# Delta rule with a convolution as side work: whose queue stores and loads, and how many steps lie between

## The chip, the cores and the metric

The kernel runs on one core of one Trainium2 chip. The metric is device time of one launch in microseconds; the times of the kernel before are the median of three runs. A trace comes from one further execution, taken with the hardware profiler. PE is TensorE, DVE VectorE, ACT ScalarE, POOL GpSimd, and SP SyncE, which here only issues transfers.

## What is computed

A trunk of two layers over 512 latent tokens (x) and 256 context tokens (ctx), 1024 wide, in float32: each layer is half a SwiGLU block, a mixer, and half a SwiGLU block. The first layer's mixer holds what the change touches: a convolution module beside a gated delta rule in both directions.

```
h    = a * sigmoid(g)                             # 512 channels
h    = depthwise_conv(h, conv_w)                  # 31 taps; latents in rows of 64 tokens
conv = silu(layer_norm(h + conv_b, ln_g, ln_b))

# delta rule, 4 heads of 128, chunks of 64 tokens, forward and backward
a_mat = where(strict, einsum(k * beta, k) * decay, 0)
t_mat = triangular_solve(a_mat + eye, eye)        # the inverse of a unit triangular matrix
v_new = u - w @ S ;  S = S * exp(g_last) + k_tail^T @ v_new ;  o = qd @ S + qk @ v_new
```

## The kernel before

One program is written out by hand. Each engine takes its instructions in the order in which the Python code emits them, and waits by semaphores for what an instruction reads. Weights come from memory through SP's queue into three raw buffers; most matrix products are split into a high and a low part and run as three matmuls.

The convolution works on four blocks (m = 0 to 3) of 128 channels. A block is a row of 918 elements: eight rows of 64 latent tokens with 15 zeros between them, then the 256 context tokens. `conv31` makes 31 taps: the first are accumulated by DVE in `ca` (L854, L857), the others are scaled by ACT (L860, L866) and added by POOL in `cp` (L845, L861, L867); at the end DVE adds both (L871) and `ca`, 888 wide with its padding, goes to the DRAM buffer `cD` (L872). It is a generator: each `yield` ends one step.

Blocks 0 and 1 run beside the projections (`conv_taps` takes some steps at the end of each projection). Blocks 2 and 3 are parked in `hD` and run as side work of the delta rule, in `side_work`: load the block (L1459, L1465), two steps, the steps of `conv31`. Then three passes over the four blocks follow (`each`): sums for the mean, centring with squares, and scaling with silu. The first two load from `cD` and pick the tokens out of the padding, in two transfers (L1446 with runs of 64 elements, L1447).

The delta rule (`gdn_ticks`) works on six chunk pairs t, two directions d and two head pairs hp. For each there are three generators:

- `prep(t, d, hp)`: the decay matrix (L1217, an exponential L1219), key and query products (L1222), the matrix N (L1227, L1230), its diagonal blocks (L1233), the first step of the inverse as a mask product and a subtraction from the identity (L1236, L1237, on DVE or POOL, with L1238 on POOL), and the transpose of that on PE (L1243), copied by ACT (L1244).
- `levels(t, d, hp)`: five doublings of the inverse: matmul, copy by ACT (L1255, L1256), a mask product by POOL (L1258), matmul, subtraction by DVE (L1266, L1269); then the last one (L1273 to L1282).
- `scan(t, d)`: the state S and the output `o_acc` of one chunk pair.

`run` advances them: in one tick every generator makes one step, in order, then the side work makes one. A first run prepares t = 0 alone. The phase t = -1 has levels(0) and prep(1); the phases t = 0 to 3 have scan(t), levels(t + 1) and prep(t + 2); the last has scan(4) and levels(5). A phase has 13 ticks. In the phases with a scan the first two preparations join at tick AFT, the other two at the tick after. Between the ticks stand matrix products of the adaptive modulation (L434, L496), whose weights SP loads (L445, L490).

Of the kernel before, what the change touches and what calls it, by code (L numbers as in the profile page):

```python
# [9 lines left out]
F32 = mybir.dt.float32  # L10
# [6 lines left out]
P = 128  # L17
# [4 lines left out]
NT = NX + NCTX  # L22
# [13 lines left out]
TAPU = 8  # L36
NLAST = 6
STG = 2
AFT = 5
NG = 3  # L40
NBG = 4
S5RD = 3
# [17 lines left out]
def trunk_kernel(  # L60
# [26 lines left out]
    def PS(name):  # L87
        return psum.tile([P, 512], F32, tag="ps", name=name)
# [708 lines left out]
    CW = 888  # L797
    NPOOL, NPOOL2 = TAPS[:2]
    hD = dram.tile([2, P, HW], F32, name="hD")
    cD = dram.tile([4, P, CW], F32, name="cD")  # L800
    sgD = dram.tile([4, P, NT], F32, name="sgD")
    kD = dram.tile([6, P, 512], F32, name="kD")
    vD = dram.tile([6, P, 512], F32, name="vD")
# [34 lines left out]
    def conv31(m, hb, ca, cp, ct):  # L838

        w = lambda j: cwT[:, j * 4 + m:j * 4 + m + 1]  # L840
        n = NPOOL if ct is not None else NPOOL2
        pj = list(range(31 - n, 31))
        cps = cp if isinstance(cp, list) else [(cp, 0, CW)]
        for c_, a, b in cps:
            GP.tensor_scalar(c_, hb[:, pj[0] + a:pj[0] + b], w(pj[0]), par[:, CONVB_O + m:CONVB_O + m + 1], ALU.mult, ALU.add)  # L845
        k = 1
        while ct is not None and k < n:
            for c_, a, b in cps:
                GP.tensor_scalar(ct[:, a:b], hb[:, pj[k] + a:pj[k] + b], w(pj[k]), None, ALU.mult)
                GP.tensor_tensor(c_, c_, ct[:, a:b], ALU.add)  # L850
            k += 1
        if ct is not None:
            yield
        V.tensor_scalar(ca, hb[:, 0:CW], w(0), None, ALU.mult)  # L854
        yield
        for j in range(1, 31 - n):
            V.scalar_tensor_tensor(ca, hb[:, j:j + CW], w(j), ca, ALU.mult, ALU.add)  # L857
            while k < n and k * (31 - n) < j * n:
                t = tmp.tile([P, SAW], F32, tag="sa", name="ctt")
                SC.activation(t, hb[:, pj[k]:pj[k] + CW], AF.Copy, scale=w(pj[k]))  # L860
                GP.tensor_tensor(cp, cp, t, ALU.add)  # L861
                k += 1
            yield
        while k < n:
            t = tmp.tile([P, SAW], F32, tag="sa", name="ctt")
            SC.activation(t, hb[:, pj[k]:pj[k] + CW], AF.Copy, scale=w(pj[k]))  # L866
            GP.tensor_tensor(cp, cp, t, ALU.add)  # L867
            k += 1
            yield
        for c_, a, b in cps:  # L870
            V.tensor_tensor(ca[:, a:b], ca[:, a:b], c_, ALU.add)  # L871
        nc.sync.dma_start(cD[m], ca)  # L872
        yield

    def conv_taps(n, tick=lambda: None):
# [267 lines left out]
    def gdn_ticks():  # L1143
# [60 lines left out]
        def prep(t, d, hp):  # L1204
            cp = ORDER[d][t]
            cols = slice(cp * P, (cp + 1) * P)
            col = lambda a, h: a[:, cp * 8 + d * 4 + 2 * hp + h:cp * 8 + d * 4 + 2 * hp + h + 1]
            DT, N, VV, Vc, bl = wk(t, d, hp)
            Ns, Nc, Vv, Vt = DT[:, :128], DT[:, 128:], Vc[:, :128], Vc[:, 128:]
            Pt = Ps[d][t % 2][:, hp * 256:hp * 256 + 256]  # L1210
            bg = DT
            if t == 0:
                bg = PS("growbc")
                for h in range(2):
                    mm(bg[:, hs(h)], col(cst[:, G], h).to_broadcast([P, P]), ident, start=True, stop=True)
            for h in range(2):
                V.scalar_tensor_tensor(DT[:, hs(h)], bg[:, hs(h)], col(cst[:, G], h), neg[:, d], ALU.subtract, ALU.min)  # L1217
            yield
            SC.activation(DT, DT, AF.Exp)  # L1219
            b0 = PS("gq")  # L1220
            for h in range(2):
                mm(b0[:, h * 256:h * 256 + 256].rearrange("p (a f) -> p a f", a=2),  # L1222
                   qk[:, 4 + 2 * hp + h, cols], qk[:, 2 * hp + h:2 * hp + h + 5:4, cols], start=True, stop=True)
            yield
            for h in range(2):
                o = h * 256
                V.scalar_tensor_tensor(N[:, hs(h)], b0[:, o + P:o + 2 * P], col(sc[:, BRK2], h), DT[:, hs(h)], ALU.mult, ALU.mult)  # L1227
            for h in range(2):
                o = h * 256
                V.scalar_tensor_tensor(Pt[:, hs(h)], b0[:, o:o + P], col(cst[:, RK], h), DT[:, hs(h)], ALU.mult, ALU.mult)  # L1230
            yield
            for q in quad:
                SC.copy(H2(Nc)[q], H2(N)[q, :, q])  # L1233
            yield
            E = V if t == 0 or hp == 0 else GP
            E.tensor_tensor(H2(Vv), H2(Nc), bl(0), ALU.mult)  # L1236
            E.tensor_tensor(H2(Vv), eye.unsqueeze(1).to_broadcast([P, 2, 64]), H2(Vv), ALU.subtract)  # L1237
            GP.tensor_tensor(H2(Ns), H2(Nc), bl(1), ALU.mult)  # L1238
            yield
            bt = PS("vt")  # L1240
            for h in range(2):
                for q in quad:
                    mm(ch(bt, h)[q], ch(Vv, h)[q], ident[q, q], start=True, stop=True)  # L1243
            SC.copy(Vt, bt[:, :128])  # L1244
            yield
# [191 lines left out]

    def side_work(cvs, cp):

        def load(m, src=None):  # L1440
            t = tmp.tile([P, SAW], F32, tag="sa", name="lnc")
            if src is not None:
                SC.dma_start(t[:, :NT], src[m])
                return t
            b = bass.AP(tensor=cD.tensor, offset=cD[m].offset, ap=[[CW, P], [79, 8], [1, 64]])
            SC.dma_start(t[:, XS].rearrange("p (r w) -> p r w", w=64), b)  # L1446
            SC.dma_start(t[:, CS], cD[m, :, 632:888])  # L1447
            return t

        def each(fn, src=None):  # L1450

            nxt = load(0, src)
            yield
            yield
            for m in range(4):
                t, nxt = nxt, load(m + 1, src) if m < 3 else None
                yield from fn(m, t)
        hb, ca = cvs
        nc.sync.dma_start(hb, hD[0])  # L1459
        yield  # L1460
        yield
        for m in (2, 3):
            yield from conv31(m, hb, ca, cp, None)
            if m == 2:
                nc.sync.dma_start(hb, hD[1])  # L1465
                yield
                yield

        def add(m, t):
            if m == 0:  # L1470
                GP.tensor_copy(acc[:, :NT], t[:, :NT])
            else:
                V.tensor_tensor(acc[:, :NT], acc[:, :NT], t[:, :NT], ALU.add)
            yield
            yield
        yield from each(add)
        for z in ("x", "c"):
            s, _ = STR[z]
            ps = PS("lnm")[:, :s.stop - s.start]
            mm(ps, ones, acc[:, s], start=True, stop=True)  # L1480
            yield
            SC.activation(rst[:, s], ps, AF.Copy, scale=1.0 / 512)

        def centre(m, t):
            V.tensor_tensor(t[:, :NT], t[:, :NT], rst[:, :NT], ALU.subtract)
            yield
            SC.dma_start(nD[m], t[:, :NT])
            q = cvs[m % 2]
            SC.activation(acc[:, :NT] if m == 0 else q[:, :NT], t[:, :NT], AF.Square)
            yield  # L1490
            if m:
                V.tensor_tensor(acc[:, :NT], acc[:, :NT], q[:, :NT], ALU.add)
        yield from each(centre)
        for z in ("x", "c"):
            s, _ = STR[z]
            n = s.stop - s.start
            ps = PS("lnv")
            mm(ps[:, :n], ones, acc[:, s], start=True, stop=True)
            yield
            rsqrt_newton(rst[:, s], ps[:, :n], 1.0 / 512, n, cvs)  # L1500

        def scaled(m, t):
            V.tensor_tensor(t[:, :NT], t[:, :NT], rst[:, :NT], ALU.mult)
            yield
            SC.activation(t[:, :NT], t[:, :NT], AF.Silu, bias=par[:, CLNB_O + m:CLNB_O + m + 1], scale=par[:, CLNG_O + m:CLNG_O + m + 1])
            SC.dma_start(nD[m, :, XS], t[:, XS])
            yield
            hi, lo = T["xnc"]
            split(hi[:, m], lo[:, m], t[:, CS])
        yield from each(scaled, nD)  # L1510
        def gates(h):
            sg = tmp.tile([P, SAW], F32, tag="sa", name="hsg")[:, :NCTX]
            SC.dma_start(sg, sgD[h, :, CS])
            return sg
        sgs = [gates(0), gates(1)]
        yield
        yield
        for h in range(4):
            sg = sgs[h]
            head_out("c", h, (4, 5), sg)  # L1520
            if h < 2:
                sgs.append(gates(h + 2))
            yield
            yield
# [762 lines left out]
```

## Time and profile before

| | |
|---|---|
| median of three runs | 2989.99 us (2988.91 to 2992.88) |
| profiled execution | 2993.55 us |
| its span, first to last instruction | 2991.8 us |
| busy: PE, DVE, ACT, POOL | 2832.5, 2005.1, 1112.4, 1087.0 us |
| PE's mean granted clock | 0.963 of full speed |
| the delta rule's stage | about 893 to 1192 us of the span |

Busy times are those of the instructions of an engine; DMA-issuing instructions and waits are not among them. A row of the timeline gives start, length, engine, line, operation, what it writes and reads, how many it merges, and in brackets the idle time of the engine ahead of it with what ended it. ACTq and SPq are the queues on which ACT and SP issue transfers. A granted clock of 1.00 is 2.4 GHz, one of 0.50 is 1.2 GHz.

### The profile page before, as it was taken

Reading aid. Unit: us, or ns where it says so; the run is one execution under the profiler, and the core shown is the slowest. Engines: PE = TensorE matmul, PEld = TensorE weight load, DVE = VectorE, ACT = ScalarE, POOL = GpSimd, SP = SyncE. Lnnn points to the kernel's source line nnn. Section 1 sums busy time; section 2 is a strip of 40 time slices with the busy share of each in tenths; the row PEclk is TensorE's granted clock in tenths of the full one; section 3 lists DMA queues with packets and bytes.
Section 4 is the critical chain, followed back from the end, with each engine's and each line's share of the span. In section 5 each row is a group of like instructions: output and inputs, shape, how many; then the busy total and the mean of one; then the engine's idle time right before and its main releaser. Section 6 shows DMA issues by size and latency. Waiting matters only on the chain.

```text
span 2991.8 us, 53430 instructions
## 1 busy us (share of the span) xinstructions
PE 2832.5 (95%) x21247; PEld 2520.0 (84%) x21247; DVE 2005.1 (67%) x3817; ACT 1112.4 (37%) x2311; POOL 1087.0 (36%) x1232
## 2 busy tenths in 40 slices
PE   7899999998997899999999999999999989899998
PEld 5799999977885677888888889799999977678997
DVE  4665666667857667658666576766666656588887
ACT  4233333343444435432222233433333332344444
POOL 0242333339307833002655232443333300046653
PEclk9899999998897898999999999999999989899999
DMA  6323341221234584332333211122221226433331
GB/s 228 104 73 127 99 127 57 65 72 43 75 106 158 200 261 150 128 83 76 105 101 103 99 54 54 50 71 62 67 76 60 71 66 211 162 105 100 113 99 64
DMA packets 306104, 308.34 MB, mean 103 GB/s; under 512 B 35053, under 2 KB 261513, under 8 KB 299200
## 3 DMA queue, kind: packets, MB, share of 16 engines
q1 hardware_dynamic: 284592, 274.89, 28.8%
q10 hardware_dynamic: 20256, 25.76, 2.6%
q8 instruction: 167, 2.74, 0.4%
q0 software_dynamic: 1008, 4.29, 0.4%
q14 instruction: 81, 0.66, 0.1%
HBM read 279.34 MB, written 25.56 MB: 102 GB/s over the span
## 4 chain that ended last, share of the span: by engine, by line
PE 73%; DVE 13%; ACT 4%; DMA 2%; POOL 2%; issue 2%; SPq 0%; ACTq 0%; POOLq 0%; DVEq 0%
PE s L369 7%; PE s L373 7%; PE s L371 7%; PE sc L371 3%; PE sc L369 3%; PE sc L373 3%; DVE wlo L163 2%; PE b L1266 1%; DVE nt L321 1%; DVE hT L688 1%; PE uac L373 1%; PE uac L371 1%; PE uac L369 1%; PE uax L369 1%; PE uax L371 1%
## 5 line engine op out<-in xcount | busy, mean ns | idle before, releaser
L163 DVE TENSOR_TENSOR wlo<-raw,whi 128x512 fp32r<-128x512 f32 (+1 forms) x793 | 596.1, 787 | 300.3 <-ACT whi L162 287.5
L162 ACT ACTIVATE whi<-raw 128x512 fp32r<-128x512 f32 (+1 forms) x813 | 476.0, 617 | 687.7 <-PE sc L371 122.4
L369 PE MATMUL s<-xnhx,whi 128*128 128x256 f32 x976 | 277.0, 284 | 0.0
L371 PE MATMUL s<-xnlx,whi 128*128 128x256 f32 x976 | 276.3, 283 | 0.4 <-DVE xnlx L364 0.4
L373 PE MATMUL s<-xnhx,wlo 128*128 128x256 f32 x976 | 276.2, 283 | 0.0
L659 POOL TENSOR_TENSOR gl<-sa,gh 128x256 fp32r<-128x256 f32 x122 | 95.8, 805 | 331.0 <-ACT gh L658 331.0
L373 PE MATMUL s<-xt,wlo 128*128 128x256 f32 x732 | 207.4, 283 | 1.8 <-POOL wlo L163 1.8
L369 PE MATMUL s<-xt,whi 128*128 128x256 f32 x732 | 207.1, 283 | 0.0
L371 PE MATMUL s<-xt,whi 128*128 128x256 f32 x732 | 207.1, 283 | 0.0
L578 POOL TENSOR_TENSOR raw<-raw 128x512 f32<-128x512 f32 x61 | 82.1, 1346 | 311.8 <-issue 286.5
L369 PEld LDWEIGHTS s<-xnhx,whi 128*128 128x128 f32 x976 | 187.2, 192 | 7.6 <-DVE hT L688 3.4
L369 PE MATMUL sc<-xnhc,whi 128*128 128x256 f32 x672 | 190.2, 283 | 0.0
L371 PE MATMUL sc<-xnlc,whi 128*128 128x256 f32 x672 | 190.2, 283 | 0.0
L373 PE MATMUL sc<-xnhc,wlo 128*128 128x256 f32 x672 | 190.1, 283 | 0.0
L371 PEld LDWEIGHTS s<-xnlx,whi 128*128 128x128 f32 x976 | 187.2, 192 | 1.5 <-DVE xnlx L364 0.6
L373 PEld LDWEIGHTS s<-xnhx,wlo 128*128 128x128 f32 x976 | 187.2, 192 | 0.0
L373 PEld LDWEIGHTS s<-xt,wlo 128*128 128x128 f32 x732 | 140.5, 192 | 2.0 <-POOL wlo L163 2.0
L369 PEld LDWEIGHTS s<-xt,whi 128*128 128x128 f32 x732 | 140.5, 192 | 0.0
L371 PEld LDWEIGHTS s<-xt,whi 128*128 128x128 f32 x732 | 140.5, 192 | 0.0
L369 PEld LDWEIGHTS sc<-xnhc,whi 128*128 128x128 f32 x672 | 129.0, 192 | 0.0
L371 PEld LDWEIGHTS sc<-xnlc,whi 128*128 128x128 f32 x672 | 129.0, 192 | 0.0
L373 PEld LDWEIGHTS sc<-xnhc,wlo 128*128 128x128 f32 x672 | 129.0, 192 | 0.0
(760 smaller groups left out, 8403.1 us busy)
## 6 DMA issues: line engine op xcount, KB each, us to landing
raw<-in_ffn_w_dram SPq DMA_DIRECT2D x176, 512.0 KB
raw<-in_w_mod_dram SPq DMA_DIRECT2D x64, 1024.0 KB
raw<-in_ffn_w_dram SPq DMA_DIRECT2D x32, 1024.0 KB
raw<-in_ffn_w_dram SPq DMA_DIRECT2D x16, 768.0 KB
raw<-in_w_mod_dram SPq DMA_DIRECT2D x16, 512.0 KB
raw<-in_e_w_in_dram SPq DMA_DIRECT2D x8, 1024.0 KB
raw<-in_e_w_out_dram SPq DMA_DIRECT2D x8, 1024.0 KB
CAD<-C ACTq DMA_DIRECT2D x4, 1152.0 KB
```

The lines of the kernel that those rows point to most:

```text
L162: SC.activation(hi, src, AF.Copy)
L163: (GP if j.slow or c in j.gp else V).tensor_tensor(lo, src, hi.bitcast(F32), ALU.subtract)
L321: V.scalar_tensor_tensor(t, hT[:, k, s], gsc[l][:, i, v, k:k + 1], rst[:, s] if src is None else src, ALU.mult, ALU.mult)
L369: mm(ps, wh, xh, start=first, stop=False)
L371: mm(ps, wh, xl, start=False, stop=False)
L373: mm(ps, wl, xh, start=False, stop=last)
L578: tt(q[2], q[0], q[2], ALU.subtract)
L659: GP.tensor_tensor(gl[:, gslot, s], sa[:, s], gh[:, gslot, s].bitcast(F32), ALU.subtract)
L688: V.scalar_tensor_tensor(hT[:, m, s], ps, ml[:, v, gate * 8 + m:gate * 8 + m + 1], hT[:, m, s], ALU.mult, ALU.add)
L1266: mm(b[q, a + h * 32:a + h * 32 + 32], ch(lhs, h)[q], half(ch(rhs, h)[q], z), start=True, stop=True)
```

## The change

The result of the convolution is stored to `cD` without the padding, in two transfers on ACT's queue in place of one on SP's; the later passes load it in one. The loads of blocks 2 and 3 go from SP's queue to ACT's, with four and three steps in place of two between load and use. The transposes of a preparation come one step after the subtraction, not in the next, and AFT is 4.

```diff
-AFT = 5
+AFT = 4
-    cD = dram.tile([4, P, CW], F32, name="cD")
+    cD = dram.tile([4, P, NT], F32, name="cD")
@@ conv31
-        nc.sync.dma_start(cD[m], ca)
+        SC.dma_start(cD[m, :, XS].rearrange("p (r w) -> p r w", w=64),
+                     bass.AP(tensor=ca.tensor, offset=ca[:, 0:1].offset, ap=[list(ca.ap[0]), [79, 8], [1, 64]]))
+        SC.dma_start(cD[m, :, CS], ca[:, 632:888])
         yield
@@ prep
             GP.tensor_tensor(H2(Ns), H2(Nc), bl(1), ALU.mult)
+            yield
             yield
             bt = PS("vt")
@@ side_work
-        def load(m, src=None):
+        def load(m, src):
             t = tmp.tile([P, SAW], F32, tag="sa", name="lnc")
-            if src is not None:
-                SC.dma_start(t[:, :NT], src[m])
-                return t
-            b = bass.AP(tensor=cD.tensor, offset=cD[m].offset, ap=[[CW, P], [79, 8], [1, 64]])
-            SC.dma_start(t[:, XS].rearrange("p (r w) -> p r w", w=64), b)
-            SC.dma_start(t[:, CS], cD[m, :, 632:888])
+            SC.dma_start(t[:, :NT], src[m])
             return t
-        def each(fn, src=None):
+        def each(fn, src=cD):
...
-        nc.sync.dma_start(hb, hD[0])
-        yield
-        yield
+        SC.dma_start(hb, hD[0])
+        for _ in range(4):
+            yield
         for m in (2, 3):
             yield from conv31(m, hb, ca, cp, None)
             if m == 2:
-                nc.sync.dma_start(hb, hD[1])
-                yield
-                yield
+                SC.dma_start(hb, hD[1])
+                for _ in range(3):
+                    yield
```

## Rows read from the trace of the kernel before

**Rows 1.** Stretches: length; busy us (instructions) PE, PEld, DVE, ACT, POOL; PEclk, DMA, GB/s

```profile
893.00:906.90 13.90, 5.74 (x36) 3.54 (x35) 7.83 (x27) 7.24 (x19) 1.76 (x2) 0.82 0.81 277
906.90:967.40 60.50, 46.47 (x703) 33.29 (x704) 48.73 (x76) 26.83 (x63) 53.60 (x52) 0.73 0.37 130
967.40:978.80 11.40, 11.19 (x211) 9.77 (x209) 5.65 (x16) 3.18 (x13) 3.96 (x8) 1.00 0.81 278
978.80:1048.30 69.50, 58.91 (x916) 45.31 (x916) 52.50 (x125) 35.68 (x100) 58.56 (x58) 0.80 0.51 182
1048.30:1136.00 87.70, 79.95 (x1260) 60.60 (x1256) 55.99 (x187) 35.83 (x119) 26.54 (x61) 0.96 0.82 263
...
sum 299.00, PE 253.25 PEld 198.44 DVE 209.08 ACT 140.03 POOL 165.06; mean PE 42.21 PEld 33.07 DVE 34.85 ACT 23.34 POOL 27.51
```

**Rows 2.** Timeline of PE: the delta rule's first matmuls and gaps at transposes

```profile
906.94 0.69 PE L1243 MATMUL vt<-ident,wk 64*64 64x64 f32 x8 [8.20 <-DVE wk L1237]
...
911.61 1.95 PE L1255 MATMUL w<-wk 64*64 64x64 f32 x32
...
948.78 0.70 PE L1243 MATMUL vt<-ident,V 64*64 64x64 f32 x8 [4.21 <-POOL V L1237]
...
981.85 1.97 PE L1255 MATMUL w<-V,wk 64*64 64x64 f32 x32 [3.26 <-DVE V L1269]
...
1017.43 0.69 PE L1243 MATMUL vt<-ident,wk 64*64 64x64 f32 x8 [4.95 <-POOL wk L1237]
...
1107.23 0.69 PE L1243 MATMUL vt<-ident,wk 64*64 64x64 f32 x8 [2.79 <-POOL wk L1237]
```

**Rows 3.** Timeline of DVE: around the convolutions' loads and the first addition

```profile
899.65 0.60 DVE L1230 SCALAR_TENSOR_TENSOR wk<-gq,cst,wk 128x128 f32<-128x128 f32 x2
904.99 0.68 DVE L854 TENSOR_SCALAR cvs<-cvs,cwT 128x888 f32<-128x888 f32 x1 [4.74 <-DMA cvs<-hD]
...
967.42 1.29 DVE L871 TENSOR_TENSOR cvs<-cvs,cvp 128x888 f32<-128x888 f32 x1 [5.61 <-POOL cvp L867]
...
978.76 0.68 DVE L854 TENSOR_SCALAR cvs<-cvs,cwT 128x888 f32<-128x888 f32 x1 [5.49 <-DMA cvs<-hD]
```

**Rows 4.** Timeline of SP's queue: the convolutions' loads and the first store

```profile
898.14 0.43 SPq L1459 DMA_DIRECT2D cvs<-hD  x1
...
968.74 0.34 SPq L872 DMA_DIRECT2D cD<-cvs  x1
...
972.61 0.38 SPq L1465 DMA_DIRECT2D cvs<-hD  x1
```

**Rows 5.** Timelines of ACT, DVE and PE around 874 us

```profile
873.55 1.64 ACT L990 ACTIVATE ts<-tt,cst 128x128 f32<-128x128 f32 x6
...
873.83 1.15 DVE L871 TENSOR_TENSOR ca<-ca,cq 128x444 f32<-128x444 f32 x2
...
874.73 0.50 PE L369 MATMUL pj0x<-xnhx,whi 128*128 128x512 f32 x1 [0.46 <-ACT ts L990]
```

**Rows 6.** Lines L1446 and L1447: issue durations in ns, minimum/median/maximum

```profile
L1446 ACTq DMA_DIRECT2D lnc<-cD x8: 366/367/382, 1047.3 to 1111.3; - x8
L1447 ACTq DMA_DIRECT2D lnc<-cD x8: 593/1377/2853, 1047.7 to 1111.8; - x8
```

**Rows 7.** Timeline of ACT: the first exponentials, and one activation-table load

```profile
895.57 1.33 ACT L1219 ACTIVATE wk<-wk 128x256 f32<-128x256 f32 x4
...
1047.43 1.28 ACT L1136 ACT_TABLE_LOAD   x1
```

**Rows 8.** Timeline of POOL: mask products of the first run

```profile
906.72 1.75 POOL L1238 TENSOR_TENSOR wk<-wk,lev 128x128 f32<-128x128 f32 x4
```

**Rows 9.** Waits from 880 to 1200: total us, times, longest

```profile
DVE acc L1473 <- DMA lnc<-cD: 10.3, 3, 5.1
```

**Rows 10.** Lines L861 and L857, 893 to 1050: durations in ns

```profile
L861 POOL TENSOR_TENSOR cvp<-cvp,ctt x28: 2058/2072/3023, 908.4 to 1036.6; 128x888 f32<-128x888 f32 x28
L857 DVE SCALAR_TENSOR_TENSOR cvs<-cvs,cwT,cvs x28: 1126/1230/2949, 910.9 to 1036.9; 128x888 f32<-128x888 f32 x28
```

## The prediction

> **What bounds the kernel now.** I read the page first. PE is busy for most of the span, so a change in another engine's work pays only where PE stands still. Every edited line but two stores belongs to the delta rule, so next I cut that stage, 893 to 1192 us, into stretches [rows 1]. The reader is to see in the sum that PE is busy 253.25 of 299 us, so 45.8 us are idle, and where: 8.2 of 13.9 before 906.9, 14.0 of 60.5 up to 967.4, almost none up to 978.8, 10.6 of 69.5 up to 1048.3, 7.8 of 87.7 after that. Two of these stretches, 906.9 to 967.4 and 978.8 to 1048.3, are the two convolutions of the side work. There POOL is the fullest engine: 53.60 of 60.50 and 58.56 of 69.50. The granted clock is 0.73 and 0.80 there: part of the time it is at 1.2 GHz and not 2.4, and in front of it stand PE's gaps.
>
> The timeline of PE says what its gaps wait for [rows 2]. Its first transposes start at 906.94 after 8.20 us, and the first level at 911.61. At 948.78 (4.21) and 1017.43 (4.95) a transpose waits for POOL's subtraction of the same tick, and at 1107.23 again (2.79). At 981.85 it waits 3.26 for DVE. (A tick is one turn of the generator `run`: each chain one step, then one step of side work.) DVE's timeline explains the first and the last gap [rows 3]: it is done with the preparation at 900.25, then sits until 904.99 for the convolution's load, with the subtractions queued behind; at 978.76 it has again sat 5.49 us for the second load. SP issued these loads at 898.14 and 972.61, the second after its wait for the store of the first result, 968.74 [rows 4]. Landing took 6.85 and 6.15 us from issue to DVE's start.
>
> **The change, part by part.** Ticks first. A preparation now has one tick more between the subtraction and its transpose. The first run has 7 ticks instead of 6, which puts the whole chain one tick later; in the phases with a scan, AFT = 4 starts the preparations a tick earlier, so their transposes stay in ticks 10 and 11 and everything ahead of them moves up one. The side work moves two ticks against its own start (4 instead of 2 after the load), and three from the second convolution on; against the chain that is one tick later for the first convolution and two for the second. Phases keep 13 ticks, and 85 steps of side work still fit into 85 ticks. I cost the extra tick, which issues nothing of the chain, at nothing.
>
> (a) Store of channel block 1, now on ScalarE. ACT is ahead of DVE here: it would start its evacuations at 873.55, while DVE's last addition ends at 874.98, and PE's next projection (874.73) waited 0.46 us for just those evacuations [rows 5]. So ACT, and PE behind it, lose 1.43 us of waiting. Then come two issues. The old loads have the same 256-byte runs: on ACT's queue the first of a pair took 0.37, the second 0.59 to 2.85, median 1.38 [rows 6]. 1.43 + 1.75 = 3.2 us; bounds 1.4 (issues beside ACT's work) and 4.7. The store of block 0 comes where PE has a whole projection queued; I take nothing, and up to 2 us if that cover is gone, since DVE rewrites the buffer.
>
> (b) Front. The load is issued by ACT behind its four exponentials, which end at 896.9 [rows 7], so 1.2 us sooner than 898.14. The subtractions no longer stand behind it, and POOL's four mask products, 1.75 us [rows 8], are done before the load lands instead of after. POOL's chain of convolution work starts 1.2 + 1.75 = 2.9 us ahead; bounds 0 and 8.2 (all of PE's gap). I take 2.9 and not the 7 that PE alone would show, because the rows name POOL as the next to be late.
>
> (c) First convolution. The transposes a tick later let PE run the next level in place of the 4.21 us, so that ACT's evacuations and scaled taps come sooner and POOL's idle time closes: 60.50 - 53.60 = 6.9 us. Bounds 0 and 6.9, I take half, 3.5: POOL's gaps are waits for ACT's taps, of which only those behind a late PE go.
>
> (d) Hand-over between the convolutions. Before, from the end of POOL's last tap (967.42, where DVE stopped waiting [rows 3]) to 978.76: 11.3 us. Afterwards: addition 1.29, two store issues 1.75, load issue 0.4, landing 6.15, together 9.6, so 1.8 us (rounded up) off; bounds 0.3 with the slowest issue and 3.5 with issues that cost nothing. Behind the waiting store on ACT stand the scan's scalings, which wait for DVE work that itself follows the addition; only the issue time reaches them. SP's own wait for the addition goes; behind it were weight loads and the decay rows, for which PE shows no gap there, so I count nothing.
>
> (e) Second convolution. Again half of POOL's idle time, 69.50 - 58.56 = 10.9, so 5.5 us (bounds 0 and 10.9); the 4.95 and the 3.26 us of PE lie in it. The chain goes on during the load, which is why the 5.49 us of DVE need not come back.
>
> (f) Two ticks. When the second convolution ends, the chain stands two ticks further on than before. A tick is worth 299/84 = 3.56 us, so 7.1 us at most, nothing if the chain itself sets the pace there; half, 3.6.
>
> (g) After 1048. For: one transfer of 3072-byte rows in place of nine pieces per partition, DVE having waited 10.3 us for these loads [rows 9], and the 2.79 us at 1107. PE's total gap up to 1136 is only 7.8 us, so most of the 10.3 is covered by PE's queue already. Against: the store of block 3 holds ACT for its issues (1.75) and a wait for DVE; and with the side work later, an exponential falls between the two reciprocal roots, one activation-table load more, 1.28 us [rows 7]. 2.8 + some against 1.75 + 1.28: nothing; bounds 5 faster (the gap of 7.8 less these two) and 8 slower (a wait of 5.61 for POOL, as DVE had at 967.42, with both issues).
>
> Sum: +3.2 - 2.9 - 3.5 - 1.8 - 5.5 - 3.6 + 0 = -14.1 us. The profiled execution took 2993.55 us (span 2991.80 and 1.75 around it), which gives 2979.5. The median of the runs is 2989.99, 3.56 below it, so I predict 2976.
>
> **A rule against it.** Rows: POOL's tap, alone or not, has a median of 2.07 us and at most 3.02, while DVE's tap goes from 1.13 to 2.95 beside it [rows 10]. So POOL is seldom held up, DVE often. The Trainium skill ("SBUF — State Buffer", section "SBUF: two separate sides") says that GpSimd and a VectorE operation with two SBUF inputs take one port pair in turn, and that the loser stands still for the whole instruction. The trace agrees for DVE and hardly for POOL. Taken strictly, POOL's idle time is filled by nobody, which is the first rival's arithmetic.
>
> **Rivals.**
> 1. The convolution keeps its pace (VectorE and POOL in each other's way): a removed wait of PE comes back as one for DVE. For it: POOL at 89% and 84%, DVE's stretched taps. Against: POOL's own gaps name ACT and PE. Terms c, e, f vanish: +3.2 - 2.9 - 1.8 = -1.5, so 2988.5: no change that can be told.
> 2. Slower: ScalarE's queue becomes the bound. One mechanism: a store stands at the head of ACT until DVE has added what POOL hands over last. Price: 4.7 at block 1, 2 x 3.2 issues at blocks 2 and 3, and 5.6 of waiting at block 3, with the level's evacuations behind it: 16.7, less b and the rest of d, some 5, so +12 or 3002. It decides once these holds pass the 17 us that b to f give. Against: at block 2 what follows waits for the same DVE anyway.
> 3. PE gets nearly all its gap back and the clock stays at 2.4 GHz: 33.0 us are idle up to 1048.3; 25 of them less the 3.2 is -22, so 2968. For it: the granted 0.73 and 0.80. Against: POOL's 53.60.
> 4. The step does not do what it says in the scan phases: transposes stay where they were, and the earlier preparation meets the scan's output on DVE. The 4.95 and half of f go: -14.1 + 5 + 1.8 = -7.3, 2982.7.
>
> **How the numbers follow.** Forecast 0.45, rivals 0.22, 0.09, 0.14, 0.10. The measurement can tell about 0.2%, 6 us, so faster is below 2984. The forecast's own range is 2969 to 2984: faster. Rival 3 is faster too, rival 4 faster in most of its spread (0.08 of 0.10). Faster 0.45 + 0.14 + 0.08 = 0.67, plus 0.02 of rival 1; same 0.22 - 0.02 + 0.02 = 0.22; slower 0.09. The range leaves out most of rival 2 and the lower half of rival 3: 2966 to 2991, where the upper end is rival 1 with block 0's 2 us.
>
> **What would show it.** Right: the first level starts some 5 us earlier against the end of the projection; no wait above 2 us before a transpose; POOL idle under 5 us and under 8 in the convolutions; PE clock above 0.85 there; the projection 3 us late near 875. Wrong: DVE's taps stretch as PE's gaps close (rival 1); ACT idle for 3 us or more at the stores with PE behind it (rival 2); transposes still waiting for POOL at the ends of the scan phases (rival 4).

## The result, and the profile after

The changed kernel takes 3005.86 us (median of six runs, 3005.5 to 3012.47), the kernel before beside it 2989.45 (2986.68 to 2992.88). The ratio is 1.0059, 95% interval 1.0046 to 1.0072: 17.6 us slower by the ratio (16.4 by the medians), where 2976 was forecast. The profiled execution took 3005.5 us, so its span differs from that of before by 11.9 us only; the stretches below account for those 11.9.

I read the same stretches first, between the same events (first transposes, end of the first convolution, start and end of the second). The columns are those of [rows 1]; the granted clock is the third number from the end.

```profile
895.00:904.50 9.50, 7.34 (x51) 5.14 (x49) 7.47 (x29) 7.26 (x19) 1.17 (x3) 1.00 0.65 190
904.50:972.60 68.10, 53.32 (x784) 37.99 (x784) 46.84 (x78) 27.60 (x65) 54.80 (x51) 0.75 0.49 179
972.60:986.60 14.00, 11.55 (x147) 10.02 (x149) 9.59 (x31) 3.45 (x13) 4.04 (x8) 0.76 0.79 238
986.60:1059.90 73.30, 61.49 (x964) 46.72 (x960) 63.85 (x143) 37.90 (x107) 61.00 (x62) 0.87 0.47 161
1059.90:1147.00 87.10, 80.30 (x1260) 62.05 (x1261) 50.60 (x163) 33.41 (x112) 23.35 (x57) 0.89 0.73 259
```

POOL's idle time was to close. It reads 68.10 - 54.80 = 13.3 us instead of 6.9 in the second row and 12.3 instead of 10.9 in the fourth, and PE's idle time 14.8 against 14.0 and 11.8 against 10.6. But the second row is no longer the first convolution: the transposes now start 7 us ahead of it, and POOL waits 6.6 of those 13.3 us for the load. From the first convolution's own start to its end, before and then after:

```profile
904.99:967.42 62.43, 46.49 (x704) 33.31 (x705) 50.60 (x79) 27.86 (x64) 55.38 (x53) 0.72 0.39 139
```

```profile
911.75:972.59 60.84, 49.53 (x712) 35.63 (x712) 44.98 (x71) 26.29 (x60) 54.11 (x49) 0.72 0.43 152
```

PE is idle for 11.3 us there instead of 15.9, POOL for 6.7 instead of 7.1, and the granted clock is the same.

Next, the timelines of the changed kernel for the marks of the work. DVE (L871 ends blocks 1 to 3, L854 starts a convolution; see [rows 3, 5]):

```profile
873.26 1.15 DVE L871 TENSOR_TENSOR ca<-ca,cq 128x444 f32<-128x444 f32 x2
...
911.75 0.68 DVE L854 TENSOR_SCALAR cvs<-cvs,cwT 128x888 f32<-128x888 f32 x1 [5.30 <-DMA cvs<-hD]
...
972.59 1.29 DVE L871 TENSOR_TENSOR cvs<-cvs,cvp 128x888 f32<-128x888 f32 x1 [7.31 <-POOL cvp L867]
...
986.63 0.68 DVE L854 TENSOR_SCALAR cvs<-cvs,cwT 128x888 f32<-128x888 f32 x1
...
1058.58 1.06 DVE L871 TENSOR_TENSOR cvs<-cvs,cvp 128x888 f32<-128x888 f32 x1
```

ACT, with its own DMA issues (ACTq):

```profile
874.45 0.37 ACTq L872 DMA_DIRECT2D cD<-ca  x1
874.85 0.60 ACTq L874 DMA_DIRECT2D cD<-ca  x1
875.55 1.66 ACT L992 ACTIVATE ts<-tt,cst 128x128 f32<-128x128 f32 x6 [2.47 <-PE tt L987]
...
901.82 0.34 ACTq L1457 DMA_DIRECT2D cvs<-hD  x1
...
911.75 1.96 ACT L860 ACTIVATE ctt<-cvs,cwT 128x888 f32<-128x888 f32 x2 [4.40 <-DMA cvs<-hD]
...
1059.68 0.38 ACTq L872 DMA_DIRECT2D cD<-cvs  x1
1060.10 1.03 ACTq L874 DMA_DIRECT2D cD<-cvs  x1
1061.22 0.60 ACT L1259 COPY wk<-w 128x128 f32<-128x128 f32 x3 [8.40 <-DVE o_acc L1372]
```

PE, its gaps and the first matmul of two scans (L1299; [rows 2] for the gaps before):

```profile
876.74 0.80 PE L369 MATMUL pj0x<-xnhx,whi 128*128 128x512 f32 x1 [2.16 <-ACT ts L992]
...
904.52 0.45 PE L1246 MATMUL vt<-ident,wk 64*64 64x64 f32 x8 [2.18 <-DVE wk L1239]
...
913.91 3.39 PE L1269 MATMUL b<-wk 64*64 64x32 f32 x64 [3.32 <-ACT wk L1259]
...
1061.54 3.63 PE L1269 MATMUL b<-wk 64*64 64x32 f32 x64 [2.85 <-ACT wk L1259]
...
1073.19 2.05 PE L1299 MATMUL ks<-S,qkT 128*128 128x128 f32 x16
...
1140.89 1.10 PE L1496 MATMUL lnv<-acc,ones 128*128 128x512 f32 x2 [2.62 <-DVE acc L1490]
...
1204.54 3.49 PE L1299 MATMUL ks<-S,qkT 128*128 128x128 f32 x16
```

The waits of transposes for POOL are gone: no row like the 4.21, 4.95 and 2.79 us of before. In their place stand waits behind ACT: 2.16 us at 876.74, 3.32 at 913.91, 2.85 at 1061.54. Ahead of the last, ACT had no work for 8.40 us: its store of block 3 waited for DVE's addition at 1058.58, and the level's copies (L1259) were queued behind the store. (The bracket names another DVE instruction, L1372; ACT's own rows show that the store went out at 1059.68, as the addition ended at 1059.64, and the copies after it.)

To compare the stretches the kernel before needs three marks more, on DVE and on PE (there the scan's line is L1296):

```profile
1047.19 1.07 DVE L871 TENSOR_TENSOR cvs<-cvs,cvp 128x888 f32<-128x888 f32 x1
```

```profile
1062.01 2.05 PE L1296 MATMUL ks<-S,qkT 128*128 128x128 f32 x16
...
1193.20 3.07 PE L1296 MATMUL ks<-S,qkT 128*128 128x128 f32 x16
```

The differences of these starts, with those of two experiments told below:

| us, from start to start | before | after | store on SP | store on SP, first run's tick out |
|---|---|---|---|---|
| block 1's addition to first convolution | 31.2 | 38.5 | 31.7 | 32.8 |
| first convolution | 62.4 | 60.8 | 60.6 | 60.5 |
| hand-over | 11.3 | 14.0 | 12.1 | 11.7 |
| second convolution | 68.4 | 72.0 | 75.5 | 71.5 |
| its end to the second scan's first L1299 | 14.8 | 14.6 | 9.8 | 9.3 |
| second scan to last scan | 131.2 | 131.4 | 134.1 | 126.1 |
| sum | 319.4 | 331.3 | 323.7 | 311.9 |

Where did PE lose it? The whole stretch, before and then after:

```profile
873.83:1193.20 319.37, 273.16 (x4188) 216.09 (x4187) 213.47 (x564) 148.30 (x433) 166.73 (x234) 0.86 0.57 188
```

```profile
873.26:1204.54 331.28, 286.12 (x4198) 225.42 (x4196) 217.48 (x563) 147.53 (x430) 165.97 (x234) 0.84 0.53 181
```

PE's idle time is the same, 46.2 and 45.2 us: the waits were moved, not removed. Its busy time is 13.0 us longer for nearly the same number of matmuls. Part of that is the clock: granted clocks of 0.86 and 0.84 are some 89 and 106 us of the stretch at 1.2 GHz. By an estimate from these, 17 us more at half the speed cost at most 8 or 9 of the 13.0 us; the rest of the longer busy time is not explained here.

### The profile page after: what moved, and what is told of

Its sections match the earlier page's. It is cut to its first block, busy times and chain, and to the rows that moved or that the text cites. A ratio compares the mean times of both kernels' runs of the same rounds, so it can differ in the third digit from the quotient of the medians.

```text
span 3003.7 us, 53437 instructions
## 1 busy us (share of the span) xinstructions
PE 2847.4 (95%) x21247; PEld 2531.1 (84%) x21247; DVE 2005.9 (67%) x3817; ACT 1112.7 (37%) x2312; POOL 1086.8 (36%) x1232
## 4 chain that ended last, share of the span: by engine, by line
PE 71%; DVE 15%; ACT 4%; POOL 2%; DMA 2%; issue 2%; ACTq 0%; POOLq 0%; DVEq 0%; SPq 0%
PE s L369 7%; PE s L373 7%; PE s L371 7%; PE sc L371 3%; PE sc L369 3%; PE sc L373 3%; DVE wlo L163 2%; PE b L1269 1%; DVE nt L321 1%; DVE hT L688 1%; PE uac L373 1%; PE uac L371 1%; PE uac L369 1%; PE uax L369 1%; PE uax L371 1%
```

## The experiments

Ratios are to the kernel before, run beside each kernel on the same chip, with 95% intervals. One profiled stretch differs from run to run by some us (two kernels with one edit between them differ by up to 5 us ahead of that edit), so times decide and traces explain. Each cost in us below is a difference of ratios of 2989.45 us, good to some 3 to 5 us. Theory A blames the stores on ScalarE's queue (A1) or the later steps (A2); theory B blames the chain's extra tick.

**The two halves.** The chain's edits alone on the kernel before:

```diff
-AFT = 5
+AFT = 4
             GP.tensor_tensor(H2(Ns), H2(Nc), bl(1), ALU.mult)
             yield
+            yield
```

> The kernel before with nothing changed but the inverse's extra tick and AFT = 4 (the two edits of the chain; DMA queues, steps and the store's layout stay as before). Theory A (the loss comes from the stores that hold ScalarE's queue and from the side work's later steps, not from the chain): same or faster, 2982 to 2990, with the 4.95 us wait of PE in the second convolution gone. Theory B (the extra tick itself costs: every phase's preparation is issued a tick earlier and takes VectorE's time from scan and levels): slower, 2995 to 3006, with phase lengths (scan to scan) that grow like those of the changed kernel.

Measured 1.0017 (1.0007 to 1.0026): 5 us slower, between the two theories. The 4.95 us wait is gone, and yet the kernel is slower. The reverse, the changed kernel without these two edits:

> The changed kernel with the chain's two edits undone (no extra tick, AFT = 5); stores, loads and steps as changed. Theory A (stores and later steps): stays slow, 3000 to 3010, since nothing that it blames is taken away. Theory B (the extra tick): back to 2986 to 2994.

1.0020 (1.0010 to 1.0030), again between the two. So the chain's edits cost 5 us by themselves and 11.7 in the changed kernel, and what is left without them is also slower than before.

**The store's queue.** In the changed kernel, both transfers of L872 and L874:

```diff
-        SC.dma_start(cD[m, :, CS], ca[:, 632:888])
+        nc.sync.dma_start(cD[m, :, CS], ca[:, 632:888])
```

> The changed kernel with only the convolution's store put back on SyncE's queue, in its new form of two transfers. Theory A1 (ScalarE's queue is held by the stores: 3.5 us at the projection near 875 and 8.4 us near 1055): 12 us back, 2992 to 2996; the idle time of ScalarE before the level's copy near 1061 goes, and the projection starts as before. Theory A2 (the later steps cost most): 3.5 us back for the projection and little else, 3000 to 3003.

1.0018 (1.0008 to 1.0029): 12 us back, as A1 said. Its marks, on DVE and PE:

```profile
869.78 1.15 DVE L871 TENSOR_TENSOR ca<-ca,cq 128x444 f32<-128x444 f32 x2
...
901.46 0.68 DVE L854 TENSOR_SCALAR cvs<-cvs,cwT 128x888 f32<-128x888 f32 x1 [2.82 <-DMA cvs<-hD]
...
1049.65 1.07 DVE L871 TENSOR_TENSOR cvs<-cvs,cvp 128x888 f32<-128x888 f32 x1
```

```profile
1059.41 2.95 PE L1299 MATMUL ks<-S,qkT 128*128 128x128 f32 x14
```

The first convolution starts 31.7 us after block 1's addition instead of 38.5, and the scan 9.8 us after the second convolution's end instead of 14.6.

**The steps.** In the changed kernel:

```diff
-        for _ in range(4):
-            yield
+        yield
+        yield
...
-                for _ in range(3):
-                    yield
+                yield
+                yield
```

> The changed kernel with two steps after each convolution load instead of four and three; all else as changed. Theory A2 (the side work that stands later against the scans costs most): 2987 to 2993, 13 us or more back, and the phase with the first scan short again. Theory A1 (stores on ScalarE): 3001 to 3006, the hold of ScalarE is still there, if at another place.

1.0055 (1.0043 to 1.0067), as slow as with the later steps. A2 falls.

**Wait or issue?** The store stays on ScalarE, both transfers one step later, behind what the level has queued:

```diff
+        yield
         SC.dma_start(cD[m, :, XS].rearrange("p (r w) -> p r w", w=64),
...
         SC.dma_start(cD[m, :, CS], ca[:, 632:888])
-        yield
```

> The changed kernel with the convolution's store still on ScalarE's queue but issued one step after the addition instead of right behind it, so that ScalarE reaches it when the addition is done; the number of steps is unchanged. Theory A1 (what costs is ScalarE's wait at the head of its queue): most of what SyncE's queue gave comes back, 2994 to 2998, and no wait of PE for ScalarE's evacuations near 876. Rival (the issues themselves and the transfers on this queue cost): 3001 to 3006, little changed.

1.0022 (1.0010 to 1.0034): 11 us back with the issues still on ScalarE. ACT's timeline at the end of the second convolution:

```profile
1058.30 0.27 ACT L1259 COPY wk<-w 128x128 f32<-128x128 f32 x1 [0.16 <-PE w L1258]
1059.43 0.38 ACTq L873 DMA_DIRECT2D cD<-cvs  x1
1059.85 2.18 ACTq L875 DMA_DIRECT2D cD<-cvs  x1
```

The level's copies now go ahead of the store, though this time the second issue took 2.18 us. So at the stores of blocks 2 and 3 the wait is what costs, not the issues. One part of the expectation failed: near 876 PE still waited 3.05 us, because block 1's steps run in one go, and the store stood in the same place on ACT.

**One edit on the kernel before.** The layout alone, with the store's two transfers on SyncE, and the layout with them on ScalarE (SC.dma_start):

```diff
-    cD = dram.tile([4, P, CW], F32, name="cD")
+    cD = dram.tile([4, P, NT], F32, name="cD")
...
-        nc.sync.dma_start(cD[m], ca)
...
+        nc.sync.dma_start(cD[m, :, CS], ca[:, 632:888])
```

> The kernel before with the unpadded layout alone: the result stored in two transfers on SyncE's queue as before, and loaded in one transfer per block for the layer norm; no other edit. Theory: the layout costs nothing and takes DVE's waits for these loads away, which PE mostly covers: 2985 to 2991. Rival (a store of 256-byte runs delays the second convolution's load behind it on the same queue): 2992 to 2997, with the handover between the convolutions longer than 11.5 us.

> The kernel before with the unpadded layout and the store on ScalarE's queue; loads, steps and chain as before. Theory A1: the store's hold of ScalarE costs without the chain's edits too: 2996 to 3002, with PE's wait near 875 of 2 to 3 us. Rival (the hold only costs where the chain's edits have brought preparations under it): 2986 to 2993.

0.9995 (0.9985 to 1.0006) and 1.0025 (1.0015 to 1.0035). The layout is worth nothing that can be told; the store on ScalarE costs 9 us without any other edit, and PE waited 3.05 us near 877 and 3.92 behind ACT at 1056.

**Chain undone and store on SyncE together:**

> The changed kernel with the chain's two edits undone and the store on SyncE's queue: what is left of the change is the layout, the later steps and the loads on ScalarE's queue. If the costs add up (chain about 5, store about 12 of which 6 are left without the chain): 2985 to 2991, no change from before. Theory A2 (the later steps cost by themselves): 2995 or more.

0.9991 (0.9976 to 1.0007): no change that can be told, as the adding up said.

**What of the chain costs?** On the kernel before, the extra tick in all preparations but the first four (the edit below, with AFT = 4); then in all, with AFT = 4 and one empty step more after the first load, which restores the position of the side work; then in all with AFT left at 5:

```diff
             yield
+            if t:
+                yield
```

> The kernel before with AFT = 4 and the inverse's extra tick in every preparation but the first four, so that the first run keeps its six ticks; DMA queues, steps and layout as before. Theory P (position: the extra tick of the first run puts the chain one tick behind the side work, and when the second convolution ends there is a tick more to do, while the waits of PE that go were covered by the convolutions' pace): the 5 us of the chain's two edits come back, 2987 to 2991, with the time from the end of the second convolution to the second scan back from 20.9 to 14 to 16 us. Theory Q (AFT = 4: preparations that start a tick earlier take VectorE's time from the scan): 2994 to 2998.

> The kernel before with the chain's two edits and one more empty step after the first convolution load (three instead of two), which puts chain and side work back into the position that they had before. Theory P: 2987 to 2991, like the kernel before. Theory Q: 2994 to 2998, like the chain's edits alone. Where the first convolution itself starts later for the extra step, 3 us more under both.

> The kernel before with the extra tick and AFT left at 5: the preparations start where they did before, and the transposes come a tick later in every phase. Theory P: like the chain's edits alone or slower, 2994 to 3002, since the position is the same. Theory Q: back to 2986 to 2991, since nothing starts earlier than before.

0.9983 (0.9973 to 0.9993), 0.9994 (0.9985 to 1.0002) and 1.0016 (1.0005 to 1.0027). Theory P holds on all three: AFT = 4 costs nothing, the first run's tick costs 10 us (1.0017 to 0.9983), and a step that restores the position takes back most of it. Without that tick the chain's edits are worth 5 us against the kernel before, so the waits that they remove did pay there. The rows that show it are the end of the second convolution and the start of the second scan. With the tick in all preparations, DVE and PE:

```profile
1042.57 1.07 DVE L871 TENSOR_TENSOR cvs<-cvs,cvp 128x888 f32<-128x888 f32 x1
```

```profile
1063.47 2.05 PE L1297 MATMUL ks<-S,qkT 128*128 128x128 f32 x16
```

and with the tick out of the first four:

```profile
1043.10 1.07 DVE L871 TENSOR_TENSOR cvs<-cvs,cvp 128x888 f32<-128x888 f32 x1
```

```profile
1058.33 2.05 PE L1298 MATMUL ks<-S,qkT 128*128 128x128 f32 x16
```

The convolution ends at the same time, and the chain then has 20.9 us to go to that scan with the tick and 15.2 without: 5.7 of the 10 us.

**Both causes taken out.** The changed kernel with the store on SyncE and the tick out of the first four:

> The changed kernel with the store on SyncE's queue and no extra tick in the first four preparations; layout, later steps, loads on ScalarE's queue and AFT = 4 as changed. If both costs found so far are the whole loss (store 12 us, the first run's tick 5 us): 2984 to 2990, not slower than the kernel before and perhaps faster. If AFT = 4 or the later steps cost something of their own: 2993 to 2998.

2981.34 us, 0.9963 (0.9949 to 0.9976), five runs: 11 us faster than the kernel before, the best version found. Its marks on DVE and PE, for the last column of the table:

```profile
870.59 1.15 DVE L871 TENSOR_TENSOR ca<-ca,cq 128x444 f32<-128x444 f32 x2
...
1047.16 1.34 DVE L871 TENSOR_TENSOR cvs<-cvs,cvp 128x888 f32<-128x888 f32 x1
```

```profile
1056.47 2.05 PE L1300 MATMUL ks<-S,qkT 128*128 128x128 f32 x16
...
1182.52 3.62 PE L1300 MATMUL ks<-S,qkT 128*128 128x128 f32 x16
```

**Do the parts add up?** The tick alone taken out of the changed kernel; only blocks 0 and 1 stored from ScalarE; and the best version with two steps after each load:

> The changed kernel with nothing undone but the extra tick of the first four preparations; stores stay on ScalarE's queue. If the tick costs what it cost on the kernel before (10 us between the two kernels that had it in all and in all but the first preparations): 2994 to 2998. If it costs what it cost with the store on SyncE's queue (16 us): 2987 to 2992. If the store's hold hides it: 3001 to 3006.

> The changed kernel with the stores of blocks 2 and 3 (the two convolutions of the delta rule) on SyncE's queue and those of blocks 0 and 1 on ScalarE's. It splits the 12 us that all four stores cost. If the projection near 875 is the larger part (load issue 4 us later, landing 2 to 3 us slower): 3000 to 3004. If the hold at the end of the second convolution is: 2995 to 2999. The term of the forecast was 3.2 us, which would be 2998.

> The kernel with the store on SyncE's queue and no extra tick in the first preparations, with two steps after each convolution load instead of four and three. If the later steps give something (the chain stands further on when the second convolution ends): 2987 to 2993, slower than with the later steps by 5 us or more. If position does not matter any more once the chain is not behind: 2979 to 2984.

1.0012 (1.0003 to 1.0022), 1.0039 (1.0026 to 1.0052) and 0.9996 (0.9986 to 1.0005). The tick costs 14 us with the store on ScalarE (1.0059 to 1.0012) and 16 with it on SyncE (1.0018 to 0.9963). The stores cost 12 us with the tick and 15 without. They divide into 6 us for blocks 0 and 1 (1.0018 to 1.0039) and 6 for blocks 2 and 3 (1.0039 to 1.0059), but the intervals of neighbours overlap, and the store issued a step later, which leaves block 1's store where it was, gave 11 us back. How the 12 divide is therefore not settled. The later steps give 10 us once the tick is out (0.9996 to 0.9963), and gave nothing while it was in.

**Why is a tick worth more than a tick?** In the fourth phase (third to fourth scan) the changed kernel and the one with the store on SyncE have the two reciprocal roots of the layer norm 13 to 14 us apart, with two activation-table loads more than without the tick, and PE waits 2.6 us for the sum of squares. Two tries, both on the kernel with the store on SyncE: the roots in one step, as below, and then also the variance matmuls one step later (the first of the two new yields stands ahead of the loop).

```diff
             mm(ps[:, :n], ones, acc[:, s], start=True, stop=True)
-            yield
-            rsqrt_newton(rst[:, s], ps[:, :n], 1.0 / 512, n, cvs)
+            pss.append((s, n, ps))
+        yield
+        yield
+        for s, n, ps in pss:
+            rsqrt_newton(rst[:, s], ps[:, :n], 1.0 / 512, n, cvs)
```

> The changed kernel with the store on SyncE's queue (the extra tick of the first run is in), and the two reciprocal roots of the layer norm's variance issued in one step instead of in two steps that follow each other, so that no preparation's exponential falls between them. If the table loads and the late second root are what the tick costs in the fourth phase: 5 us less than with the store on SyncE's queue alone, 2988 to 2992, and the phase between the third and the fourth scan back from 52.9 to 47 to 49 us. If the position itself costs the 16 us: 2993 to 2998.

> The changed kernel with the store on SyncE's queue (the extra tick of the first run is in); the two variance matmuls of the layer norm are issued together one step later than now, and the two reciprocal roots together in the step behind them, in the same number of steps. Theory W (what the tick costs in the fourth phase is PE's 2.63 us wait for the sum of squares, with the level's matmuls queued behind it, and the half clock after it: 3.78 us against 1.99 for eight Gram matmuls): 2990 to 2994, with no wait before the variance matmul and the phase between the third and the fourth scan at 47 to 50 us. Rival (the wait moves elsewhere; position costs whatever stands there): 2995 to 3000, the phase at 52 us or more.

1.0027 (1.0017 to 1.0037) and 1.0018 (1.0007 to 1.0030). In the first the roots stand together (ACT) and PE still waits:

```profile
1142.81 1.28 ACT L275 ACT_TABLE_LOAD   x1
1144.11 1.05 ACT L275 ACTIVATE rst<-lnv,eps_c 128x512 f32<-128x512 f32 x2
```

```profile
1132.92 2.90 PE L1497 MATMUL lnv<-acc,ones 128*128 128x512 f32 x4 [2.63 <-DVE acc L1490]
```

The phase still takes 55.8 us, so the table loads are not the cause. In the second the wait is gone:

```profile
1137.18 1.45 PE L1498 MATMUL lnv<-acc,ones 128*128 128x512 f32 x4
```

The phase is down to 49.2 us from 52.9, the one ahead of it is 3.6 longer, and the time is that of the kernel it was built on. I take neither as shown. That the position costs 10 us on the kernel before and 14 to 16 in the changed one is shown; by which waits stays open. It is not one place: on the kernel before 5.7 us lie behind the second convolution, while with the store on SyncE (the last two columns of the table) it is 0.5 us there, 4.0 in the second convolution and 8.0 behind the second scan.

**The loads' queue.** The best version with the convolution's loads on SyncE as well:

> The kernel with the store on SyncE's queue and no extra tick in the first preparations, with the convolution's loads on SyncE's queue as well. It isolates the loads' queue. If the load from ScalarE's queue gives nothing (the convolution started 30 to 33 us after block 1's addition from either queue): 2978 to 2985, the same. If the subtractions that no longer stand behind the load matter (the forecast's term b and part of d, 4.7 us): 2985 to 2990.

0.9976 (0.9964 to 0.9987). The intervals overlap: the loads from ScalarE may give 4 us or nothing.

## Why the prediction was wrong

**The extra tick "at nothing" is the step that failed most.** The prediction costed "the extra tick, which issues nothing of the chain, at nothing", and took it into account only as one of three ticks in (f). It costs 10 us on the kernel before and 14 to 16 in the changed one. On the kernel before, the second convolution ends at the same time with and without the tick, and the chain then has 5.7 us more to go; the rest of the cost is measured and not placed.

**(a) and (g), the stores, were the second.** Priced at 3.2 us for block 1 and nothing net for block 3, they cost 12 to 15. Rival 2 named the mechanism and the places (projection, and a store at the head of ACT until DVE adds): it priced 16.7 us of holds. It had 0.09, because I set its gains against it and left the tick out. That its 3002 came near is partly luck: of the gains that it set off, b and d gave nothing, and of the tick it said nothing.

At block 1, PE's wait was 2.16 us (3.05 in later kernels) instead of 0.46, and the projection ended 4.2 us later against block 1's addition, so (a) was too small. The kernel with only blocks 0 and 1 stored from ScalarE shows it without the other stores (DVE, ACTq, DVE):

```profile
869.48 1.15 DVE L871 TENSOR_TENSOR ca<-ca,cq 128x444 f32<-128x444 f32 x2
...
898.77 0.34 ACTq L1458 DMA_DIRECT2D cvs<-hD  x1
...
906.51 0.68 DVE L854 TENSOR_SCALAR cvs<-cvs,cwT 128x888 f32<-128x888 f32 x1 [2.88 <-DMA cvs<-hD]
```

The load with all four stores on SyncE:

```profile
893.61 0.34 ACTq L1457 DMA_DIRECT2D cvs<-hD  x1
```

It goes out 29.3 us after block 1's addition started instead of 23.8, lands in 7.74 us instead of 7.85, and the convolution starts 5.3 us later, which is the size of the 6 us that the time shows. In the changed kernel the load went out after 28.6 us and landed in 9.93. Block 0's store shows no cost of its own: the kernel before and the changed one add it at 799.6 and 800.0 us and start the next projection within 0.6 us of each other. At block 3, 8.40 us of ACT's idle time, with 2.85 us of PE's wait behind it, replaced the 1.75 plus "a wait for DVE".

These two together, the tick and the stores, are 28.7 us (from 1.0059 to 0.9963), of which 3.2 had been forecast. The remaining -11 stands against a forecast of -17.3 for (b) to (f).

**(b), front: no gain.** The first level started at 906.85, some 8 us earlier against the end of the projection, and then waited 3.32 us for ACT, which sat behind the late load. With the store on SyncE the convolution starts 31.7 us after the addition against 31.2: against that addition the load went out 0.5 us earlier, where 1.2 was forecast, and it took 1.0 us longer to land.

**(c) and (e), the convolutions: no net gain in the changed kernel, as rival 1 said, but not by its mechanism.** The first takes 60.5 to 60.8 us instead of 62.4, the second 71.5 to 75.5 instead of 68.4. Rival 1's sign was that DVE's taps stretch. They hardly did ([rows 10] before):

```profile
L861 POOL TENSOR_TENSOR cvp<-cvp,ctt x28: 2056/2078/2904, 913.5 to 1045.2; 128x888 f32<-128x888 f32 x28
```

```profile
L857 DVE SCALAR_TENSOR_TENSOR cvs<-cvs,cwT,cvs x28: 1124/1292/2937, 912.5 to 1048.9; 128x888 f32<-128x888 f32 x28
```

DVE's median tap rose from 1.23 to 1.29 us and POOL's from 2.07 to 2.08. By the Trainium skill ("SBUF — State Buffer", "SBUF: two separate sides") one of the two stands still for the other's whole instruction. The ranges above allow it for DVE (1.12 to 2.94 us) more than for POOL (2.06 to 2.90), before as after, and no run shows it as the cause of the convolutions' length.

The idea of (e) did hold on the kernel before. With the tick out of the first four preparations, POOL's waits for ACT's taps in the second convolution fall from 6.9 us to 1.3 (total, times, longest; before and then there):

```profile
POOL cvp L861 <- ACT ctt L860: 6.9, 3, 4.9
```

```profile
POOL cvp L861 <- ACT ctt L860: 1.3, 2, 1.1
```

That convolution starts at

```profile
978.52 0.68 DVE L854 TENSOR_SCALAR cvs<-cvs,cwT 128x888 f32<-128x888 f32 x1 [6.32 <-DMA cvs<-hD]
```

and takes 64.6 us instead of 68.4, so 3.8 of the 5.5 forecast came. What goes with the longer one in the changed kernel is the number of steps after its load: 69.8 to 75.5 us in every version here with three, 64.4 to 69.5 in every one with two. The prediction has no term for that; which work makes it longer stays open.

**(d), hand-over: no gain.** 11.7 to 14.0 us instead of 9.6. The first convolution's end and the next one's start are joined by three steps of the generator, and a load that lands early waits for them: in the kernel with the store on SyncE, as in the changed one, DVE starts it with no wait for a transfer. The best version with two steps has a hand-over of 5.5 us and is 10 us slower all the same, so this stretch alone does not set the time.

**(f), the ticks: the row agrees, the gain is not shown.** 14.8 became 9.3 to 9.8 us behind the second convolution with the store on SyncE, 5.0 to 5.5 us where 3.6 was forecast; in the changed kernel block 3's hold took the same 4.8 back. But the convolution ahead of it is longer: from its start to the second scan it is 83.3 us before, 85.2 with the store on SyncE, and 80.8 with the tick out as well. In time, the later steps gave nothing with the tick and 10 us without it, so a number near 3.6 in one row is partly luck.

**The clock** was to rise to 0.85 in both convolutions. It was 0.75 and 0.87 in the rows, 0.72 from the first convolution's own start as before, and 0.89 behind them where it had been 0.96.

## What to carry to other kernels

- A DMA issue that waits for another engine's result is an instruction of the engine that issues it: everything queued behind waits too. Look up what stands behind it, at every place where it is issued, before it is moved to a compute engine; or issue it a step later, when the result is there. The Trainium skill ("DMA: Bandwidth & Descriptors", "Issuing engines are not separate DMA queues") says that another issuing engine saves only sequencer time. The trace agrees: the issues of these stores took 0.36 to 1.53 us each on SyncE's queue, and that is all that moving them could save there, against 8.40 us in which ScalarE had no work.
- Where two streams are stepped in lockstep, an empty step in one is not free. Ask how many steps are left when the slower stream ends, and price each of them; the mean length of a step, 3.6 us, was far too little here (10 to 16).
- A wait that goes pays in full only if what follows it was the bound. Compare the duration of the stretch's slowest stream in both kernels before counting PE's gaps as time.

## What the runs showed of the hardware

- The first convolution load took 6.5 us from issue to use on ScalarE's queue in the version without the chain's edits and with the store on SyncE, and 9.93 us in the changed kernel, where it went out 5 us later against block 1's addition. The core's DMA engines were 0.96 and 0.95 busy in the two, so their busy share does not tell them apart. What the load met was not isolated.
- The second issue of the store's pair took 0.59 to 2.18 us on ScalarE's queue and 0.57 to 1.53 us on SyncE's.
- PE's idle time of 46.2 and 45.2 us went with busy times of 273 and 286 us for nearly the same matmuls and granted clocks of 0.86 and 0.84: the sum of the gaps did not give the time here.
